# q and k of three heads ahead of the rest, seven products for every v, gate and SwiGLU pair, and a quad's first product copied into the bank of its second

## The chip, the cores and the metric

One core of a Trainium2 chip runs the kernel. The metric is the device time of one execution in microseconds (us). Engines: TensorE (PE), VectorE (DVE), ScalarE (ACT), GpSimd (POOL) and SyncE (SP, which issues most loads).

## What is computed

One layer of an encoder on x (512 tokens x 1024, float32), cut to its core:

```python
h = rmsnorm(x, g_mix)
xc, gb, gc, q, k, v, g_sw, gate_a, gate_r = split(h @ w_in)          # 1024 -> 3x1024, 1024, 1024, 2048, 2048, 1024, 1024
y_a = (gb * conv3(gc * xc)) @ w_a_out
q, k = rotary(q) * 256**-0.5, rotary(k)                              # 4 heads of 256; v: 4 heads of 512
ret  = retention(q, k, v, log_sigmoid(dec_f)) + reversed_strict_retention(q, k, v, log_sigmoid(dec_b))
y_r  = (groupnorm(ret) * g_ret * silu(g_sw)) @ w_r_out
x = x + (sigmoid(gate_a) * y_a + sigmoid(gate_r) * y_r) @ w_o
h2 = rmsnorm(x, g_ffn)
x = x + (silu(h2 @ w_ff_gate) * (h2 @ w_ff_up)) @ w_ff_down          # 1024 -> 2816 -> 1024
y = rmsnorm(x, g_final)
```

## The kernel before

Every operand of a matmul is split into a rounded high part and the rest (`split`: a cast on ACT, L171, and a subtraction on DVE, L172), and each product is three matmuls, high x high, high x low and low x high (`mm3`, L284 to L286; `prod`, L325, with 256 columns; `prod_tm`, L369, with 512). Weights come by SP's queue into `raw` tiles (10 buffers), and are split into `whi` and `wlo` (5 buffers of 128x1024, a "unit"), two units ahead of use. `plan()` lists the weights in the order of use. The order of instructions on each engine is that of a scheduler in the framework, which works from the program's order and the buffers; each engine then runs its own list in order.

A "quad" is a product of a 2x2 block matrix of activations and weights by Strassen's seven products: forms of the weights (b11, t1, t2, b21, t3, t4, b22) against forms of the activations (a11, s1, s2, a12, s3, a22, s4). A t-form of weights is made by DVE additions of two `raw` tiles (L244). `strassen` does it with 512 columns (v beside the gate of a head, the two branch gates, and w_ff_down), `fm_quad` with 256 (the convolution's inputs), `begin`, `second` and `pair` with 256 for SwiGLU. Three results are read while their bank goes on accumulating: ACT copies the bank to SBUF (`snap`, L376). The first product a11 is snapped too, and DVE adds it to a12's bank (L390, L339, L1018).

The order of the work: eight warm-up matmuls; v and gate of head 0 as plain products on x times gain, not yet normalised, since the reciprocal roots of the tokens (`rstd_tokens`, then `rstd_row` after the v product) are still computed; then x is normalised and the s-forms are made; q and k of head 0 (`do_qk`, rotated on DVE from PSUM by the table `rcs`); for heads 1 to 3 a quad for v and gate, and q and k; two quads for the branch gates; the decay tables (`decays`, with the logarithm `lgam` computed by small DVE steps on `lw`, L517 to L525, then Exp on ACT, L541); convolution, retention, output projections, w_o with a norm and transposes (`tr_o`, L910); SwiGLU, whose first pair of 256-column blocks is made by eight plain products (`first_pair`), the other ten by quads; w_ff_down in three parts; the last norm. v, gates, q and k are stored by POOL's queue (`store`, L566) from nine temporaries of 128x512 (`t512`).

## Time and profile before

| | us |
|---|---|
| runs | 1044.6 median of 3 (1043.32 to 1044.88) |
| profiled execution, its time | 1043.97 |
| its span, first to last instruction | 1042.2 |
| granted TensorE clock, mean | 0.998 |
| first matmul of the work | 6.67 |
| last matmul | 1033.33 |
| quad of head 1, 2, 3: start | 77.81, 137.65, 198.09 |

The span begins with the first instruction and ends with the last; 1.8 us of the execution's time lie around it. In a profile a line such as L369 is a line of the kernel; a helper's line stands for all that call it. Matmuls overlap, so the listed duration of one is longer than what it adds; the difference of the starts of neighbours is what it adds.

### The profile page before, as it was taken

To read this page: it belongs to the slowest core of one execution; us is meant where nothing else is said; L and a number is where in the kernel's file an instruction comes from. 1 tells how busy PE (TensorE), PEld (TensorE's weight loads), DVE (VectorE), ACT (ScalarE), POOL (GpSimd) and SP (SyncE) were. 2 spreads that over 40 slices of the span, in tenths; PEclk is the share of its full clock that TensorE was granted. 3 is DMA by queue.
4 is the path that set the end of the run, shared out by engine and by line. 5 is a ranking of instruction groups with operands and counts; after the bars stand their busy time and mean duration, and the time that the engine had idled before them with its cause. 6 is when DMAs were issued, how large, how long until landed. Compare 5 with 4: busy or idle time off the path is not lost.

```text
span 1042.2 us, 14832 instructions
## 1 busy us (share of the span) xinstructions
PE 1028.3 (99%) x5664; PEld 897.0 (86%) x5664; DVE 875.5 (84%) x1127; ACT 523.4 (50%) x698; POOL 107.7 (10%) x180
## 2 busy tenths in 40 slices
PE   8999999999999999999999999999999999999996
PEld 7788888888888998888888888889998999899985
DVE  6999786858787888697989998669998899889995
ACT  6546745452656545243443234355555565556553
POOL 0121111111111004202011000000002000110011
PEclk9999999999999999999999999999999999999999
DMA  9635638173645576919176535630319322663322
GB/s 325 223 117 201 236 123 281 71 254 119 199 141 182 169 284 233 341 42 358 42 283 247 205 111 173 236 113 28 92 45 275 117 85 78 193 152 102 122 35 87
DMA packets 49688, 175.07 MB, mean 168 GB/s; under 512 B 6480, under 2 KB 6480, under 8 KB 46288
## 3 DMA queue, kind: packets, MB, share of 16 engines
q1 hardware_dynamic: 36592, 131.12, 36.9%
q0 software_dynamic: 13024, 43.00, 12.9%
q8 instruction: 44, 0.72, 0.3%
q14 instruction: 28, 0.23, 0.1%
HBM read 135.56 MB, written 38.54 MB: 167 GB/s over the span
## 4 chain that ended last, share of the span: by engine, by line
PE 77%; issue 9%; DVE 7%; DMA 3%; POOL 2%; ACT 1%; SPq 0%; POOLq 0%; DVEq 0%; ACTq 0%
PE bank L369 29%; PE bank L325 27%; PE bank L285 7%; PE bank L284 7%; PE bank L286 7%; DVE wlo L172 1%; POOL z L566 1%; DVE big L185 1%; DMA big<-ql 1%; DMA big<-xT 1%; DMA z<-t 1%; DMA tab<-tab 0%; DVE big L172 0%; DVE t L464 0%; DVE big L175 0%
## 5 line engine op out<-in xcount | busy, mean ns | idle before, releaser
L171 ACT CAST whi<-raw 128x1024 fp32r<-128x1024 f32 (+1 forms) x281 | 288.6, 1032 | 302.7 <-PE bank L369 66.4
L172 DVE TENSOR_TENSOR wlo<-raw,whi 128x1024 fp32r<-128x1024 f32 (+1 forms) x281 | 335.8, 1202 | 108.8 <-ACT whi L171 107.8
L325 PE MATMUL bank<-xform,whi 128*128 128x256 f32 x1440 | 260.3, 283 | 0.0
L325 PEld LDWEIGHTS bank<-xform,whi 128*128 128x128 f32 x1440 | 224.8, 192 | 0.7 <-ACT t L376 0.6
L325 PE MATMUL bank<-xform,wlo 128*128 128x256 f32 x720 | 203.7, 283 | 0.0
L369 PE MATMUL bank<-whi,big 128*128 128x512 f32 x548 | 172.4, 390 | 0.0
L244 DVE TENSOR_TENSOR raw<-raw 128x1024 f32<-128x1024 f32 (+1 forms) x124 | 148.5, 1205 | 1.8 <-DMA raw<-wquad 0.4
L325 PEld LDWEIGHTS bank<-xform,wlo 128*128 128x128 f32 x720 | 138.2, 192 | 0.0
L369 PEld LDWEIGHTS bank<-whi,big 128*128 128x128 f32 x548 | 102.7, 188 | 22.4 <-DVE big L172 0.6
L369 PE MATMUL bank<-wlo,big 128*128 128x512 f32 x274 | 106.7, 389 | 0.0
L369 PE MATMUL bank<-whi,xform 128*128 128x512 f32 x320 | 101.2, 389 | 0.3 <-ACT t L376 0.3
L284 PE MATMUL bank<-whi,big 128*128 128x512 f32 x240 | 94.3, 395 | 1.8 <-ACT big L174 1.8
L285 PE MATMUL bank<-wlo,big 128*128 128x512 f32 x240 | 94.3, 393 | 0.0
L286 PE MATMUL bank<-whi,big 128*128 128x512 f32 x240 | 93.4, 392 | 0.0
L284 PE MATMUL bank<-big,whi 128*128 128x512 f32 x224 | 87.1, 389 | 0.0
L285 PE MATMUL bank<-big,whi 128*128 128x512 f32 x224 | 87.1, 389 | 0.0
L286 PE MATMUL bank<-big,wlo 128*128 128x512 f32 x224 | 87.1, 389 | 0.0
L376 ACT COPY t<-bank 128x512 f32<-128x512 f32 x96 | 55.5, 585 | 35.8 <-PE bank L369 17.2
L369 PEld LDWEIGHTS bank<-whi,xform 128*128 128x128 f32 x320 | 60.1, 188 | 13.1 <-ACT t L376 0.7
L369 PE MATMUL bank<-wlo,xform 128*128 128x512 f32 x160 | 62.2, 389 | 0.0
L369 PEld LDWEIGHTS bank<-wlo,big 128*128 128x128 f32 x274 | 51.4, 188 | 10.5
L284 PEld LDWEIGHTS bank<-whi,big 128*128 128x128 f32 x240 | 45.5, 190 | 12.5 <-ACT big L174 2.1
(173 smaller groups left out, 1398.6 us busy)
## 6 DMA issues: line engine op xcount, KB each, us to landing
raw<-wquad SPq DMA_DIRECT2D x124, 512.0 KB, 4.4
raw<-wpack SPq DMA_DIRECT2D x58, 512.0 KB, 4.9
z<-t POOLq DMA_DIRECT2D x24, 256.0 KB, 4.9
zform<-z POOLq DMA_DIRECT2D x6, 1024.0 KB, 6.2
v<-t POOLq DMA_DIRECT2D x16, 256.0 KB, 5.0
sg<-t POOLq DMA_DIRECT2D x16, 256.0 KB, 3.3
qh<-t POOLq DMA_DIRECT2D x16, 256.0 KB, 2.6
ql<-t POOLq DMA_DIRECT2D x16, 256.0 KB, 2.7
```

What stands on the lines that cost most here:

```text
L171: nc.scalar.copy(hi, src)
L172: nc.vector.tensor_tensor(out=lo, in0=src, in1=hi.bitcast(F32), op=ALU.subtract)
L185: nc.vector.transpose(o[:, :, :, b, :], i[:, :, :, q, :])
L244: nc.vector.tensor_tensor(out=t, in0=t, in1=raws[quad, more, u][:, 0:n], op=ALU.add)
L284: nc.tensor.matmul(ps, lh, rh, start=first, stop=False)
L285: nc.tensor.matmul(ps, lh, rl, start=False, stop=False)
L286: nc.tensor.matmul(ps, ll, rh, start=False, stop=last)
L325: nc.tensor.matmul(o, l[:, c], r[:, k], start=start and s == 0 and k == 0 and i == 0, stop=stop and k == 3 and i == 2, skip_group_check=True)
L369: nc.tensor.matmul(pss[tt], l, r[:, c], start=start and k == 0 and i == 0, stop=stop and k == n - 1 and i == 2, skip_group_check=True)
L376: nc.scalar.copy(t, ps)
L566: nc.gpsimd.dma_start(dst, t)
```

## The change

q and k of heads 0 to 2 are computed first, four banks to a head, on x times gain without the tokens' norm; ACT copies them to SBUF (`early`), and they are rotated later, half a head in each of the first six quads, by a table `rcn` that holds the tokens' norm too. v and gate of head 0 become a quad, as does SwiGLU's first pair. In each quad ACT copies a11's bank into another bank (`seed`), and a12 accumulates onto that copy; the addition on DVE is gone. The decay tables are made before the quads, with two tables of differences, eight Exps, and stores by POOL's queue. At the start the small columns come by ACT's queue, x ahead of weights, in larger transfers, and the first cast of weights is on DVE. The core of the diff, with a few comments put in:

```diff
@@ plan(): order of the weights
-    for c in (C_V, C_G):
+    for h in range(EARLY):                       # EARLY = 3
         for r in (0, 512):
-            b("w_in", r, 4, c, 512)
+            b("w_in", r, 4, (C_Q + h * QK, C_K + h * QK), 512)
     for h in range(HEADS):
-        if h:
-            quad(C_V + h * VD, C_G + h * VD)
-        a("w_in", C_Q + h * QK)
-        a("w_in", C_K + h * QK)
+        quad(C_V + h * VD, C_G + h * VD)
+        if h >= EARLY:
+            a("w_in", C_Q + h * QK)
+            a("w_in", C_K + h * QK)
...
-    f(0, "b11", "b21", "b12", "b22")
+    f(0, "b11", "b21")
     f(1, "b11", "b21")
+    f(2, "b11")
     for q0, n in FF_PARTS:
-        for q in range(max(q0, 1), q0 + n):
+        for q in range(q0, q0 + n):
...
-            if q + 1 < NQ:
+            if 1 < q < NQ - 1:
                 f(q + 1, "b11")
@@ prefetch_block()
-        for c in range(2 * per):
-            nc.sync.dma_start(st[c // per][:, c % per * m:(c % per + 1) * m], wpack[i][:, c * m:(c + 1) * m])
+        for c, (o, n) in enumerate(((0, 512), (512, 512), (QH, QH)) if pieces > 2 else ((0, QH), (QH, QH))):
             if loads:
                 loads(c)
+            nc.sync.dma_start(st[o // QH][:, o % QH:o % QH + n], wpack[i][:, o:o + n])
...
+                round = None if made else nc.vector.tensor_copy
+                made.append(split(st[half][:, sl], hi[:, sl], lo[:, sl], round=round))
@@ quads
+    def seed(ps, t=None):
+        t = t or bank()
+        nc.scalar.copy(t, ps)
+        return t
 def fm_quad(...):                                # strassen() likewise
-        a, d, b = bank(), bank(), bank()
+        a, d = bank(), bank()
         prod(w(), forms["a11"], a, True)
-        p1 = snap(a)
+        b = seed(a)
         prod(w(), forms["s1"], d, True)
         prod(w(), forms["s2"], a, False)
         u2 = snap(a)
-        prod(w(), forms["a12"], b, True)
-        nc.vector.tensor_tensor(out=p1, in0=b, in1=p1, op=ALU.add)
-        ev11(p1)
+        prod(w(), forms["a12"], b, False)
+        ev11(b)
@@ start
+    cols_sb = const.tile([P, N_COLS], F32, name="cols_sb")
+    nc.scalar.dma_start(cols_sb, cols)
...
-    prefetch(4, load_x, split_x)
+    prefetch(4, lambda c: load_x(c, 1 + c // 2), split_next)
+    prefetch(2, lambda c: load_x(4 + 2 * c, 2), lambda c: split_two(4 + 2 * c))
...
+    for h in range(EARLY):
+        pss = [bank() for _ in range(4)]
+        for kk in range(8):
+            if kk % 4 == 0:
+                c = Chunk()
+            if (h, kk) == (0, 7):
+                ss.rstd_tokens()
+            if (h, kk) == (1, 1):
+                rrow = snap(ss.rstd_row())
+                xg = quarters()                  # x times gain and rrow, and its split, as before
...
+            for m in range(4):
+                mm3(pss[m], c.w(kk % 4, m * P, P), act_pair(xu, kk), kk == 0, kk == 7)
+        t = bigtile()
+        for m in range(4):
+            nc.scalar.copy(t[:, m, :], pss[m])
+        early.append(t)
@@ decays: called before the four heads instead of after the gates' quads
+        for h in range(HEADS):
+            f, g = t512(), t512()
+            nc.scalar.activation(f, d[0], AF.Exp, scale=lgam[:, h:h + 1])
+            nc.scalar.activation(g, d[1], AF.Exp, scale=lgam[:, 4 + h:5 + h])
+            nc.vector.tensor_tensor(out=f[:, 0:P], in0=f[:, 0:P], in1=g[:, 384:512], op=ALU.mult)
+            store(tabs[h][:, 0:384], g[:, 0:384])
+            store(tabs[h][:, 384:896], f)
@@ rotation of the early heads: rcn = rcs * rrow, one half head in each quad
+    def turn_one():
+        if held:
+            h, j = held.pop(0)
+            rotate(h, j, early[h][:, 2 * j, :], early[h][:, 2 * j + 1, :], rcn)
...
+                if tt and o:                     # in do_quad's eviction of the sixth product
+                    turn_one()
     for h in range(HEADS):
-        if h:
-            do_quad(vd[h], sgd[h], AF.Silu)
-        do_qk(h)
+        do_quad(vd[h], sgd[h], AF.Silu)
+        if h >= EARLY:
+            do_qk(h)
@@ w_o: after the evictions of token blocks 1 and 3
+        if nb in (1, 3):
+            prefetch()
@@ SwiGLU (first_pair() is gone)
     def begin(q):
...
-        st["p1"] = snap(st["a"])
+        st["p1"] = seed(st["a"], (po[0][1], po[0][2], po[1][2])[q] if q < 3 else None)
     def second(q):
-        b = bank()
         _, (w,) = take()
-        prod(w, XF[1, 0], b, True)
-        g = heads_of[q]["p1"]
-        nc.vector.tensor_tensor(out=g, in0=b, in1=g, op=ALU.add)
+        prod(w, XF[1, 0], heads_of[q]["p1"], False)
     def pair(q):
...
-        if q + 1 < NQ:
+        if 1 < q < NQ - 1:
             begin(q + 1)
...
-    first_pair()
+    begin(0)
+    second(0)
+    tr_o(NB - 1, hs[NB - 1])
+    XF.update(sums(xf32[0, 0], xf32[1, 0], xf32[0, 1], xf32[1, 1]))
     begin(1)
     second(1)
+    begin(2)
     for q0, n in FF_PARTS:
-        for q in range(max(q0, 1), q0 + n):
+        for q in range(q0, q0 + n):
             pair(q)
@@ tail
-            put(held.pop())
+            with tc.issue_after(add.ins), tc.issue_after(square.ins):
+                put(held.pop())
```

How it moves instructions, at three places. On TensorE around the row of reciprocal roots: `bank<-t512,ones_r` (L493 before, L509 and L510 after) are the matmuls that spread the roots over the partitions. Before, the first of them follows straight on the first product that comes after the small `rstd_tokens` matmuls:

```order
L284 MATMUL bank_260<-whi_151,big_96 128x512
L285 MATMUL bank_260<-wlo_152,big_96 128x512
L286 MATMUL bank_260<-whi_151,big_98 128x512
L493 MATMUL bank_405<-t512_377,ones_r_83 128x512
L284 MATMUL bank_410<-whi_315,big_95 128x512
L285 MATMUL bank_410<-wlo_316,big_95 128x512
```

Afterwards, the second head's first matmuls stand ahead of it:

```order
L294 MATMUL bank_365<-big_96,wlo_281 128x512
L292 MATMUL bank_366<-big_96,whi_280 128x512
L293 MATMUL bank_366<-big_98,whi_280 128x512
L294 MATMUL bank_366<-big_96,wlo_281 128x512
L509 MATMUL bank_324<-t512_342,ones_r_85 128x512
L510 MATMUL bank_324<-t512_343,ones_r_85 128x512
L292 MATMUL bank_363<-big_96,whi_280 128x512
L293 MATMUL bank_363<-big_98,whi_280 128x512
```

Between the last `rstd_tokens` matmul and the first row matmul there are 12 matmuls of 512 columns before, and 24 after; the low half's matmul moves up to the high half's.

On ACT, at the start of the first quad of the program. Before (head 1's quad; the rows are the end of q and k of head 0, `t<-t` their rotated halves, and `t_800`, `t_802` the snaps of a11):

```order
46 L171 CAST xform<-big 128x1024
47 L171 CAST whi<-raw 128x1024 x2
48 L171 CAST t_655<-t_650 128x512
49 L171 CAST t_666<-t_661 128x512
50 L171 CAST whi<-raw 128x1024 x2
51 L171 CAST t_739<-t_734 128x512
52 L171 CAST whi<-raw 128x1024 x2
53 L171 CAST t_750<-t_745 128x512
54 L171 CAST whi<-raw 128x1024
55 L376 COPY t_800<-bank 128x512
56 L376 COPY t_802<-bank 128x512
```

After (head 0's quad): L531 and L532 are the Exps of the decays, L586 the copies of the early heads' banks, `xform` the s-forms, L340 the seeds. Just ahead of these rows stand two more Exps (36, 37) and, in row 35, the cast of t1's first unit:

```order
38 L531 ACTIVATE t_718<-t_705,lgam 128x512
39 L532 ACTIVATE t_719<-t_709,lgam 128x512
40 L531 ACTIVATE t_725<-t_705,lgam 128x512
41 L532 ACTIVATE t_726<-t_709,lgam 128x512
42 L531 ACTIVATE t_732<-t_705,lgam 128x512
43 L532 ACTIVATE t_733<-t_709,lgam 128x512
44 L586 COPY big<-bank 128x512 x2
45 L174 CAST xform<-big 128x1024
46 L586 COPY big<-bank 128x512 x2
47 L174 CAST xform<-big 128x1024 x3
48 L174 CAST whi<-raw 128x1024
49 L340 COPY bank<-bank 128x512 x2
```

Eight Exps, four copies and the casts of the four s-forms now stand between the cast of t1's first unit and that of its second, in row 48.

On TensorE in SwiGLU, from s2 (t2's product) to s3 (t3's). Before, in the first pair that is a quad, s2 is `bank_6221<-xform_6146` and the rows of `bank_6381` are the next pair's first product:

```order
L325 MATMUL bank_6221<-xform_6146,wlo_6251 128x256
L325 MATMUL bank_6221<-xform_6146,whi_6250 128x256 x2
L325 MATMUL bank_6221<-xform_6146,wlo_6251 128x256
L325 MATMUL bank_6381<-xform_5790,whi_6313 128x256 x2
L325 MATMUL bank_6381<-xform_5790,wlo_6314 128x256
L325 MATMUL bank_6381<-xform_5790,whi_6313 128x256 x2
```

After, in pair 0, s2 is `bank_5970<-xform_6045`, and s3, `xform_6041`, is the next row:

```order
L333 MATMUL bank_5970<-xform_6045,whi_6114 128x256 x2
L333 MATMUL bank_5970<-xform_6045,wlo_6115 128x256
L333 MATMUL bank_5970<-xform_6045,whi_6114 128x256 x2
L333 MATMUL bank_5970<-xform_6045,wlo_6115 128x256
L333 MATMUL bank_5970<-xform_6041,whi_6148 128x256 x2
L333 MATMUL bank_5970<-xform_6041,wlo_6149 128x256
```

The 13 matmuls of the next pair between s2 and s3 are gone there; between s3 and a22 stand 6 matmuls instead of 11. `begin(0)`, the copy and `second(0)` follow one another with nothing between.

More of the change, by code (lines that the diff above doesn't have):

```diff
@@ L177, in split @@
                 op0=ALU.mult, op1=ALU.subtract)
+        return first
     def transpose(out, src):
@@ L379, in strassen @@
     def strassen(n, forms, ev11, ev21, ev22, ev12):
-        a, d, b = ([bank(), bank()] for _ in range(3))
+        a, d = ([bank(), bank()] for _ in range(2))
         prod_tm(n, forms["a11"], a, True)
-        p1 = [snap(x) for x in a]
+        b = [seed(x) for x in a]
         prod_tm(n, forms["s1"], d, True)
@@ L498, in block_kernel, with decays @@
     for k in range(8):
-        ss.add(xs[k // 4][:, k % 4, :])
+        with tc.issue_after(made[min(k + 1, 3)].ins):
+            ss.add(xs[k // 4][:, k % 4, :])
     ss.split()
+    def decays():
+        d = []
+        for base, op in ((0, ALU.max), (-384, ALU.min)):
+            delta = t512(mybir.dt.int32)
+            nc.gpsimd.iota(delta, pattern=[[1, 512]], base=base, channel_multiplier=-1)
+            d.append(t512())
+            nc.vector.tensor_scalar(out=d[-1], in0=delta, scalar1=0.0, scalar2=None, op0=op)
+        for h in range(HEADS):
[5 more added lines that the diff above has]
+            store(tabs[h][:, 384:896], f)
@@ new lines, in keep, with store @@
+    def keep(dst, src):
+        hi, lo = t512(F32R), t512(F32R)
+        split(src, hi, lo)
+        for d, t in zip(dst, (hi, lo)):
+            store(d, t.bitcast(F32))
+    def store(dst, t):
+        nc.gpsimd.dma_start(dst, t)
+    rrow = None
+    early = []
+    for h in range(EARLY):
[8 more added lines that the diff above has]
+                xg = quarters()
+                for k in range(8):
+                    xk = xs[k // 4][:, k % 4, :]
+                    nc.vector.scalar_tensor_tensor(out=xk, in0=xk, scalar=gmix[:, k:k + 1], in1=rrow,
+                                                   op0=ALU.mult, op1=ALU.mult)
+                for i in range(2):
+                    for k in (0, 2):
+                        split(xs[i][:, k:k + 2, :], xg[0][i][:, k:k + 2, :], xg[1][i][:, k:k + 2, :])
+            for m in range(4):
[4 more added lines that the diff above has]
+        early.append(t)
@@ new lines, in form_tile, with sums @@
+    def form_tile():
+        t = big.tile([P, 2, 4, 256], F32R, tag="big", name="xform", padded_shape=[P, 2, 4, 256])
+        return t[:, 0], t[:, 1]
+    def sums(a11, a12, a21, a22):
+        out = {}
+        for name, o, in0, in1, op in (
+                ("s1", a22, a21, a22, ALU.subtract), ("s3", a21, a11, a21, ALU.subtract),
+                ("s2", a11, a22, a11, ALU.subtract), ("s4", a12, a12, a11, ALU.add)):
+            nc.vector.tensor_tensor(out=o, in0=in0, in1=in1, op=op)
+            out[name] = form_tile()
+            split(o, *out[name])
+        return out
@@ L503, in block_kernel @@
+    xf = sums(*(xs[i][:, :, o:o + 256] for o in (0, 256) for i in range(2)))
+    for n, i, o in (("a11", 0, 0), ("a12", 1, 0), ("a22", 1, 256)):
+        xf[n] = tuple(t[i][:, :, o:o + 256] for t in xg)
+    xforms = {n: of(t) for n, t in xf.items()}
     dec = const.tile([P, 8], F32, name="dec")
@@ L608, in block_kernel, with rotate @@
-    for n, i, o in (("a11", 0, 0), ("a12", 1, 0), ("a22", 1, 256)):
-        xf[n] = tuple(t[i][:, :, o:o + 256] for t in xg)
-    xforms = {n: of(t) for n, t in xf.items()}
+    def rotate(h, j, t1, t2, table):
+        cos, sin = table[:, 0, :], table[:, 1, :]
+        for i, (c1, c2, op) in enumerate(((cos, sin, ALU.subtract), (sin, cos, ALU.add))):
+            a, b = t512(), t512()
+            nc.vector.tensor_tensor(out=a, in0=t1, in1=c1, op=ALU.mult)
+            nc.vector.tensor_tensor(out=b, in0=t2, in1=c2, op=ALU.mult)
+            nc.vector.tensor_tensor(out=a, in0=a, in1=b, op=op)
+            keep([t[:, 2 * j + i, :] for t in qkd[h]], a)
@@ L612, in do_qk @@
+    rcn = misctile(D, "rcn").rearrange("p (i n) -> p i n", i=2)
+    for i in range(2):
+        nc.vector.tensor_tensor(out=rcn[:, i, :], in0=rcs[:, i, :], in1=rrow, op=ALU.mult)
+    held = [(h, j) for h in range(EARLY) for j in range(2)]
+    def turn_one():
+        if held:
+            h, j = held.pop(0)
+            rotate(h, j, early[h][:, 2 * j, :], early[h][:, 2 * j + 1, :], rcn)
     def do_qk(h):
@@ L1093, in to_y @@
         done[nb] += 1
+        return add, square
     def rms(nb):
```

160 lines of the change are left out of this document (42 added, 118 removed).

## The prediction

> **What bounds the kernel now.** I read the page's busy times first, then the list of waits of TensorE, then stretches of the timeline. One line of busy times:
>
> ```profile
> PE 1028.3 (99%) x5664; PEld 897.0 (86%) x5664; DVE 875.5 (84%) x1127; ACT 523.4 (50%) x698; POOL 107.7 (10%) x180
> ```
>
> TensorE is busy for 99% of the span of 1042.2 us. Everything that it waits for, in the list of its waits (bank, line <- releaser: us in total, times, longest):
>
> ```profile
> PE bank L284 <- ACT big L174: 1.8, 1, 1.8
> PE bank L493 <- ACT t L171: 1.7, 1, 1.7
> PE bank L415 <- DVE lw L508: 1.0, 1, 1.0
> PE bank L285 <- DMA big<-ql: 0.4, 1, 0.4
> PE bank L369 <- ACT t L376: 0.3, 1, 0.3
> ```
>
> These five rows add up to 5.2 us. So a matmul that is removed anywhere is worth its full spacing, as long as no new wait fills the place; and the only wait in mid-kernel worth removing is L493. The spacing is the difference of starts, not the listed duration, since neighbours overlap. Timeline of TensorE, start and duration in us, first for 512 columns and then for 256 ("x2" is two matmuls in one row):
>
> ```profile
> 499.77 0.39 PE L286 MATMUL bank<-whi,big 128*128 128x512 f32 x1
> ...
> 501.13 0.39 PE L286 MATMUL bank<-whi,big 128*128 128x512 f32 x1
> ...
> 733.72 0.28 PE L325 MATMUL bank<-xform,wlo 128*128 128x256 f32 x1
> 733.84 0.40 PE L325 MATMUL bank<-xform,whi 128*128 128x256 f32 x2
> ```
>
> 499.77 to 501.13 is six spacings (five matmuls stand between the two rows), 0.2267 us each; 733.72 to 733.84 is one, 0.120.
>
> **The change, term by term,** against the profiled execution (1043.97 us; the median of the runs is 1044.6, 0.6 above it).
>
> *Head 0's v and gate by seven products.* Two plain products of 96 matmuls (8 row blocks x 4 banks x 3) become seven of 24: 192 becomes 168. 24 x 0.2267 = **-5.44 us**. [...] q and k of heads 0 to 2 keep their 288 matmuls; they only move.
>
> *SwiGLU's first pair by seven products.* Eight products of 24 matmuls of 256 columns become seven. 24 x 0.120 = **-2.88 us**.
>
> *The row of reciprocal roots.* Now, on TensorE:
>
> ```profile
> 28.58 0.49 PE L284 MATMUL bank<-whi,big 128*128 128x512 f32 x1
> ...
> 31.21 0.39 PE L286 MATMUL bank<-whi,big 128*128 128x512 f32 x1
> 33.33 0.50 PE L493 MATMUL bank<-t,ones_r 128*128 128x512 f32 x1 [1.72 <-ACT t L171]
> ...
> 35.04 0.50 PE L494 MATMUL bank<-t,ones_r 128*128 128x512 f32 x1
> 35.38 0.39 PE L286 MATMUL bank<-whi,big 128*128 128x512 f32 x1
> ```
>
> From 31.21 to 35.38 lie eight spacings, which would take 1.81 and take 4.17: 2.36 lost. The chain that is waited for ends on ACT and DVE here:
>
> ```profile
> 32.66 0.62 ACT L171 CAST t<-t 128x512 fp32r<-128x512 f32 x1 [6.03 <-DVE lw L518]
> ...
> 34.30 0.68 DVE L172 TENSOR_TENSOR t<-t,t 128x512 fp32r<-128x512 f32 x1
> ```
>
> The hi half is there at 33.28, 4.7 us after 28.58. After the change 24 matmuls (5.44 us) stand between instead of 12, so the first of the two row matmuls finds its operand. The lo half comes 6.4 us after 28.58 now, but one us of that passes between the cast's end and the subtraction's start at 34.30, while DVE did other work; the small steps of the decays' logarithm no longer share DVE there. I take **-2.2**, between 0 (the lo half again late by a weight and a table's worth) and -2.36.
>
> *The first quad.* Durations by form that price this and what follows:
>
> ```profile
> L172 DVE TENSOR_TENSOR wlo<-raw,whi 128x1024 fp32r<-128x1024 f32 x270 | 328.4, 1223 | 101.9 <-ACT whi L171 101.0
> L171 ACT CAST whi<-raw 128x1024 fp32r<-128x1024 f32 x270 | 281.9, 1049 | 293.0 <-PE bank L369 64.7 <-PE bank L286 53.9 <-PE bank L325 45.7
> L376 ACT COPY t<-bank 128x512 f32<-128x512 f32 x96 | 55.5, 585 | 35.8 <-PE bank L369 17.2 <-PE bank L325 15.6 <-PE bank L286 2.5
> L619 DVE TENSOR_TENSOR t<-bank,rcs 128x512 f32<-128x512 f32 x16 | 11.0, 686 | 1.1 <-PE bank L286 1.1
> L525 DVE TENSOR_SCALAR lgam<-lgam 128x4 f32<-128x4 f32 x1 | 0.2, 170 | 0.0
> ```
>
> Let T be the end of the 288 early matmuls. ACT runs in its order: the cast of t1's first unit, eight Exps, four copies of the last early banks with four casts of forms, then the cast of t1's second unit (the order on ACT is shown with the change). The Exps wait for lgam, whose last steps on DVE stand behind that first unit. The unit's buffer comes free when the third head's second quarter is done, at T-10.9 (48 matmuls left). Then a cast of 1.05, a subtraction 1.22, an addition 1.22 and seven small steps of 0.2: T-6.0. Two Exps, at a copy's 0.59 each, bring T-4.8; the last Exp takes a buffer whose store must land first. The nearest stores, with us from issue to landing at the row's end:
>
> ```profile
> v<-t POOLq DMA_DIRECT2D x16, 256.0 KB, 5.0
> sg<-t POOLq DMA_DIRECT2D x16, 256.0 KB, 3.3
> qh<-t POOLq DMA_DIRECT2D x16, 256.0 KB, 2.6
> ```
>
> With 2.6 to 5.0 to land and 0.6 for the last Exp, ACT is free at T-1.6 to T+0.8. From there copies 4 x 0.59 and casts 4 x 1.05 take 6.5, and DVE needs two subtractions (2.4) more, for the fourth form and t1's second unit: 9.0 in all, where TensorE wants them at T+8.4 (36 matmuls and one). Lateness -1.0 to +1.4. I take **+1.2**, near the upper end, because t2's casts and subtractions stand behind these in the same two orders; bounds 0 to +4 (the late 1.4 again for t2, and an Exp or two). [...]
>
> *The quads' new load.* Each of six quads now carries one half head's rotation: eight DVE operations of 0.69 (5.5 us), less two additions (1.4). Both stretches below are TensorE at full work: one head's q and k with preparation of forms, and a quad (us, then busy time and count by engine: PE, PEld, DVE, ACT, POOL):
>
> ```profile
> 35.00:77.80 42.80, 42.76 (x188) 35.40 (x189) 41.51 (x45) 22.92 (x28) 7.62 (x13) 1.00 0.43 143
> 137.70:176.30 38.60, 38.30 (x169) 31.41 (x168) 28.95 (x32) 22.44 (x28) 6.42 (x12) 1.00 0.65 211
> ```
>
> A quad on DVE becomes 14 subtractions and 8 additions of weights (26.9), four of results (2.8) and the rotation (5.5): 35.2 in 38.1. DVE stood at 41.5 of 42.8 above without a wait of TensorE. The seeds on ACT take the place of snaps and have two products (10.9 us) before they are used. I count **0** (to +4), covered by DVE's remaining 2.9 us a quad.
>
> *The copies into banks where nothing stands between.* The last product of a kind that is read and then accumulated further, in a conv quad now, with six matmuls between:
>
> ```profile
> 348.41 0.28 PE L325 MATMUL bank<-xform,wlo 128*128 128x256 f32 x1
> ...
> 349.13 0.28 PE L325 MATMUL bank<-big,wlo 128*128 128x256 f32 x1
> 349.37 0.50 PE L325 MATMUL bank<-big,whi 128*128 128x256 f32 x2
> 349.71 0.28 PE L325 MATMUL bank<-big,wlo 128*128 128x256 f32 x1
> ```
>
> (Between the first two rows stand five matmuls, of another product.) The reading copy takes 0.59 (L376 above), and the bank is written again 0.96 after the last matmul's start; the two gaps cost 0.22 (349.13 to 349.71 is 0.58 for three spacings). Without the six it is 0.72 more, 0.94; with two, 0.70. By the new order: SwiGLU begin(0) goes straight into second(0), 0.94; in pair 0 s2 into s3, 0.94; s3 into a22 with six, 0.22; in pair 1 two, 0.70, and six, 0.22. In pair 0 the next pair's first weights (two matmuls put ahead) wait for the buffer of t1, just read, and a cast of 1.05, behind another: 1.3. Together **+4.3**, bounds +1.5 (only those the copy forces) to +6.5 (s1's form, which now has three products, 8.6 us, ahead of it instead of a whole pair, is late too). What goes from this stretch is a gap of 0.25, in place of 0.36 for three:
>
> ```profile
> 738.88 0.78 PE L325 MATMUL bank<-xform,whi 128*128 128x256 f32 x3
> 739.49 0.28 PE L325 MATMUL bank<-xform,wlo 128*128 128x256 f32 x1
> ```
>
> **-0.25**. The last conv quad loses seven score matmuls that stood between s3 and a22: **+0.72** (0 to 0.94).
>
> *Start, tail, table stores:* the first loads are bigger and x comes first, yet the same 2 MB (four row blocks of x and of weights) must land before the third and fourth block can be multiplied; 0, within about one copy of 0.6 either way. The eight table stores join a queue whose engine is 10% busy, and the last output store is moved behind an addition that waits for the last matmul anyway: 0.
>
> Sum: -5.44 - 2.88 - 2.2 + 1.2 + 4.3 - 0.25 + 0.72 = -4.55, so 1043.97 - 4.55 = **1039.4 us**.
>
> **The rivals.**
>
> *No new waits.* The scheduler's order keeps other work at all these places, or ACT answers faster: 1043.97 - 5.44 - 2.88 - 2.2 - 0.25 = 1033.2. For it speaks that TensorE is kept at 99% today; against it, the same copy already costs 0.22 behind six matmuls.
>
> *The temporaries hold DVE in the quads (the other side).* Rotation adds four stores a quad, all through nine temporaries of 128x512. A rotation row on DVE that waits for such a store holds the subtraction for t2's first unit, queued behind it; TensorE waits for that. From the end of the quad's last evictions the row comes 9.6 us after, where 11.1 are to be had: 1.5 to spare. A store of v lands 5.0 after issue, so a row held 3 us would cost 1.5 in each of six quads, 9 in all: 1048.4. It decides beyond 2.7 us. For: v's 5.0 against 2.6 of qh. Against: POOL is idle nine tenths of the time, and the list of waits names no store.
>
> *Upper bounds together in one place: pair 0.* If s1's form and first quad both come at their bounds, +2.2 and +2.8 on top: 1044.4, no change. For: DVE is at 95% in that stretch:
>
> ```profile
> 740.00:779.00 39.00, 39.00 (x288) 36.87 (x287) 37.24 (x49) 22.94 (x34) 0.00 (x0) 1.00 0.17 54
> ```
>
> *The row's wait stays.* The reciprocal row still waits, in another head: +2.2, 1041.6.
>
> **How the numbers follow.** The forecast's case 0.60 (1036.5 to 1042); no new waits 0.13; the row's wait stays 0.05; pair 0 and first quad at their bounds 0.13 (about 1042.5 to 1046); temporaries 0.09. Faster by over 0.2% (under 1042.5, about what can be told from no change at 1044.6) holds the first three, 0.78; same 0.13; slower 0.09. The range 1034 to 1045 leaves out most of the no-wait case and the temporaries.
>
> **What would show it.** Right: 24 fewer matmuls of each width; L509 without a wait; one gap of 1 to 2 us in the first quad on a weight or form; three gaps near 0.9 and one near 1.3 at SwiGLU's first two pairs, named after copies by ACT. Wrong: TensorE waits of over 1 us on DVE in the second to sixth quad, rotation rows on DVE that wait for DMAs, or a third row block at the start that waits for its load beyond 15 us.

## The result, and the profile after

The changed kernel takes 1038.12 us (median of 4 runs, 1036.39 to 1038.57), the kernel before 1044.11 (4 runs): ratio 0.9943, 95% interval 0.993 to 0.9956. That is 5.99 us, 0.57% faster; 1039.4 was forecast. The profiled execution took 1038.05 us with a span of 1036.3. One execution further down, one of b2, took 3046.7 us (a span of 3044.7 at a granted clock of 1.000), and is left out.

The page's line of busy times after:

```profile
PE 1021.7 (99%) x5616; PEld 890.2 (86%) x5616; DVE 878.9 (85%) x1121; ACT 541.1 (52%) x735; POOL 114.8 (11%) x189
```

48 matmuls fewer, and TensorE is still busy for 99%. The list of TensorE's waits after (bank, line <- releaser: us in total, times, longest):

```profile
PE bank L333 <- ACT t L390: 1.5, 3, 0.7
PE bank L333 <- ACT bank L340: 1.5, 1, 1.5
PE bank L292 <- DVE whi L174: 1.1, 1, 1.1
PE bank L430 <- DVE lw L616: 1.0, 1, 1.0
PE bank L333 <- ACT whi L174: 1.0, 1, 1.0
PE bank L383 <- ACT bank L340: 0.4, 1, 0.4
PE bank L383 <- DVE wlo L175: 0.4, 1, 0.4
PE bank L333 <- DVE xform L175: 0.2, 1, 0.2
```

The waits grew from 5.2 to 7.1 us, although the 1.7 of the reciprocal row are gone: new are six rows: three name ACT's copies (L390, and L340, the copy from bank to bank), one a cast of weights, two late lo halves. The list leaves out idle time that it does not put down to a releaser, so below I use the timeline: the difference of starts, less 0.227 us for 512 columns or 0.120 for 256.

TensorE's timeline after, places in the order of the program (start, duration in us):

```profile
5.97 1.62 PE L292 MATMUL bank<-big,whi 128*128 128x512 f32 x3 [1.15 <-DVE whi L174]
...
9.93 0.40 PE L292 MATMUL bank<-big,whi 128*128 128x512 f32 x1
...
26.99 0.17 PE L491 MATMUL bank<-ones_r,t 128*128 128x2 f32 x1
...
33.16 0.40 PE L294 MATMUL bank<-big,wlo 128*128 128x512 f32 x1
33.39 0.39 PE L509 MATMUL bank<-t,ones_r 128*128 128x512 f32 x1
...
82.62 0.61 PE L383 MATMUL bank<-whi,xform 128*128 128x512 f32 x2
83.60 0.50 PE L383 MATMUL bank<-wlo,xform 128*128 128x512 f32 x1 [0.36 <-DVE wlo L175]
...
340.61 0.28 PE L333 MATMUL bank<-big,wlo 128*128 128x256 f32 x1
341.32 0.51 PE L333 MATMUL bank<-big,whi 128*128 128x256 f32 x2 [0.43 <-ACT t L390]
...
696.37 0.28 PE L333 MATMUL bank<-xform,wlo 128*128 128x256 f32 x1
698.15 0.50 PE L333 MATMUL bank<-xform,whi 128*128 128x256 f32 x2 [1.50 <-ACT bank L340]
...
714.31 0.28 PE L333 MATMUL bank<-xform,whi 128*128 128x256 f32 x1
715.56 0.82 PE L333 MATMUL bank<-xform,whi 128*128 128x256 f32 x3 [0.97 <-ACT whi L174]
...
769.07 0.50 PE L383 MATMUL bank<-whi,big 128*128 128x512 f32 x1 [0.42 <-ACT bank L340]
```

The row of reciprocal roots (33.39) follows its neighbour by 0.23: no wait. The first quad waits once, 0.53 plus 0.10 for the slow first spacing behind it, on a lo half. The first quad of the convolution waits 0.59 plus 0.10 on a snap. SwiGLU's begin(0) and second(0) are 1.78 apart instead of the 0.96 that the copy in the conv quad of before took (348.41 to 349.37); where pair 0 waits for its borrowed weights the starts are 1.25 apart, with slow spacings behind.

What stands ahead of that copy, from ACT's timeline:

```profile
696.57 1.04 ACT L174 CAST whi<-raw 128x1024 fp32r<-128x1024 f32 x1 [0.53 <-PE bank L333]
697.52 0.58 ACT L340 COPY bank<-bank 128x512 f32<-128x512 f32 x1
```

A cast of weights that waited for TensorE started 0.2 us after the product's last matmul did; the copy stood behind it.

The end of the span, TensorE and then DVE after:

```profile
1028.74 0.39 PE L383 MATMUL bank<-whi,big 128*128 128x512 f32 x1
```

```profile
1029.16 0.69 DVE L1115 TENSOR_TENSOR big<-bank,big 128x512 f32<-128x512 f32 x1 [0.64 <-PE bank L383]
1029.77 0.74 DVE L1140 SCALAR_TENSOR_TENSOR big<-big,fin,gf 128x512 f32<-128x512 f32 x1
```

and before:

```profile
1033.33 0.39 PE L369 MATMUL bank<-whi,big 128*128 128x512 f32 x1
```

```profile
1034.79 0.75 DVE L1111 SCALAR_TENSOR_TENSOR big<-big,fin,gf 128x512 f32<-128x512 f32 x1 [0.65 <-POOL fin L1099]
1035.46 0.68 DVE L1087 TENSOR_TENSOR big<-bank,big 128x512 f32<-128x512 f32 x1
```

Before, the last addition (L1087) began 2.13 us after the last matmul's start, because DVE stood in front of it with a scaling that waited for POOL. After, it begins 0.42 after, and the scaling comes behind it. From the last matmul's start to the end of the span it is 8.87 before and 7.56 after.

The ledger, in us, by differences of starts in the two profiled executions (a row is good to 0.1 or 0.2):

| place | predicted | measured |
|---|---|---|
| 24 + 24 matmuls | -8.32 | -8.32 |
| start (first matmul 6.67, now 5.97) | 0 | -0.75 |
| row of reciprocal roots | -2.2 | -2.33 |
| first quad (+0.63; a wait of 0.57 in head 2's quad is gone) | +1.2 | +0.06 |
| quads 2 to 6 | 0 | 0 |
| convolution | +0.72 | +0.54 |
| SwiGLU, pairs 0 and 1 (0.43 before, 6.08 after) | +4.05 | +5.65 |
| w_ff_down, first part | not priced | +0.89 |
| a load of q's lo half (-0.70), w_o (+0.34) | not priced | -0.36 |
| tail | 0 | -1.3 |
| sum | -4.55 | -5.92 |

### The profile page after: what moved, and what is told of

It reads as the page before. It is cut to its first block, busy times and chain, and to the rows that moved or that the text cites. A ratio compares the mean times of both kernels' runs of the same rounds, so it can differ in the third digit from the quotient of the medians.

```text
span 1036.3 us, 14743 instructions
## 1 busy us (share of the span) xinstructions
PE 1021.7 (99%) x5616; PEld 890.2 (86%) x5616; DVE 878.9 (85%) x1121; ACT 541.1 (52%) x735; POOL 114.8 (11%) x189
## 4 chain that ended last, share of the span: by engine, by line
PE 65%; issue 22%; POOL 5%; DVE 5%; ACT 2%; DMA 1%; POOLq 0%; SPq 0%; ACTq 0%; DVEq 0%
PE bank L333 23%; PE bank L383 13%; PE bank L294 10%; PE bank L292 10%; PE bank L293 9%; DVE wlo L175 1%; DVE raw L252 1%; POOL sg L559 1%; POOL v L559 1%; POOL qh L559 1%; POOL ql L559 1%; ACT whi L174 1%; DVE big L600 1%; POOL tab L559 0%; POOL lw L617 0%
## 5 line engine op out<-in xcount | busy, mean ns | idle before, releaser
L175 DVE TENSOR_TENSOR wlo<-raw,whi 128x1024 fp32r<-128x1024 f32 (+1 forms) x290 | 344.2, 1199 | 98.5 <-ACT whi L174 97.8
L383 PE MATMUL bank<-whi,big 128*128 128x512 f32 x596 | 188.0, 390 | 0.5 <-ACT bank L340 0.4
L252 DVE TENSOR_TENSOR raw<-raw 128x1024 f32<-128x1024 f32 (+1 forms) x136 | 161.6, 1203 | 1.4
L383 PEld LDWEIGHTS bank<-whi,big 128*128 128x128 f32 x596 | 111.6, 188 | 25.5 <-ACT bank L340 0.9
L383 PE MATMUL bank<-whi,xform 128*128 128x512 f32 x384 | 121.2, 389 | 0.0
L383 PE MATMUL bank<-wlo,big 128*128 128x512 f32 x298 | 116.0, 389 | 0.0
L383 PEld LDWEIGHTS bank<-whi,xform 128*128 128x128 f32 x384 | 72.1, 188 | 15.0
L383 PE MATMUL bank<-wlo,xform 128*128 128x512 f32 x192 | 74.8, 390 | 0.4 <-DVE wlo L175 0.4
L292 PE MATMUL bank<-whi,big 128*128 128x512 f32 x176 | 69.0, 392 | 0.0
L293 PE MATMUL bank<-wlo,big 128*128 128x512 f32 x176 | 68.5, 389 | 0.0
L294 PE MATMUL bank<-whi,big 128*128 128x512 f32 x176 | 68.2, 390 | 0.1
L390 ACT COPY t<-bank 128x512 f32<-128x512 f32 x77 | 45.0, 585 | 43.0 <-PE bank L333 21.0
L292 PEld LDWEIGHTS bank<-big,whi 128*128 128x128 f32 x224 | 42.5, 190 | 10.2 <-ACT big L177 1.4
```

What stands on the lines that cost most here:

```text
L175: nc.vector.tensor_tensor(out=lo, in0=src, in1=hi.bitcast(F32), op=ALU.subtract)
L252: nc.vector.tensor_tensor(out=t, in0=t, in1=raws[quad, more, u][:, 0:n], op=ALU.add)
L292: nc.tensor.matmul(ps, lh, rh, start=first, stop=False)
L293: nc.tensor.matmul(ps, lh, rl, start=False, stop=False)
L294: nc.tensor.matmul(ps, ll, rh, start=False, stop=last)
L383: nc.tensor.matmul(pss[tt], l, r[:, c], start=start and k == 0 and i == 0, stop=stop and k == n - 1 and i == 2, skip_group_check=True)
```

## The experiments

My theory after the result: the matmuls saved are worth their spacing; head 0's seven products pay, SwiGLU's first pair costs more than it saves, because copies on ACT stand bare between products; the copies as seeds bring nothing by themselves; the tail's new order is a gain that I had not priced. The rivals were, for each part, that it does the opposite or nothing. The runs a, b and c were made on three different chips, each beside the kernel before (1043.71, 1043.29 and 1042.7 us); across the letters, compare ratios.

**a1, the tail alone undone.**

```diff
-            with tc.issue_after(add.ins), tc.issue_after(square.ins):
-                put(held.pop())
+            put(held.pop())
```

> Only the tail's order is undone: the last output's store and scaling may again be issued ahead of the last addition. Theory: the changed kernel's tail (7.6 us from the last matmul's start to the end of the span, against 8.9 before) is shorter because DVE no longer holds the last addition behind a scaling that waits for POOL; then this run is 1.3 us longer than the changed kernel, 1039.4. Rival: the tail is shorter for another reason (a store that lands sooner), and nothing changes: 1038.1.

Measured: 1038.27 (1038.17 to 1038.33), ratio 0.9947 (0.9932 to 0.9962). Its last matmul and the last addition:

```profile
1027.02 0.39 PE L383 MATMUL bank<-whi,big 128*128 128x512 f32 x1
```

```profile
1028.49 0.75 DVE L1140 SCALAR_TENSOR_TENSOR big<-big,fin,gf 128x512 f32<-128x512 f32 x1 [0.65 <-POOL fin L1128]
1029.16 0.68 DVE L1115 TENSOR_TENSOR big<-bank,big 128x512 f32<-128x512 f32 x1
```

The addition is 2.14 behind the matmul's start again, with the scaling in front, and the tail takes 9.2 us (to 1036.2) against 7.56. So the mechanism stands and is worth 1.65 us here. The total alone hides it: 1038.27 is as long as the changed kernel's 1038.12. This kernel reached its last matmul 1.72 us sooner, and that came entirely from the start: its first two-column matmul (L491), after 84 large ones, began at 25.26 where the changed kernel's began at 26.99. That is the start, which differs from run to run (see b1 and the end). By the ratios it is 1.7 us slower than the control b1 (0.9947 against 0.9931), but the intervals overlap: what shows the mechanism is the order on DVE and the tail's length, not the total.

**b1, the changed kernel once more,** as a control on another chip.

> The changed kernel once more, beside the others, to see how far its own runs spread. In the traces so far TensorE leaves half rate 2.1 to 4.0 us after its first matmul of the work, which makes up to 1.7 us of difference between runs of one kernel. Theory: that is all of the spread (1036.4 and 1038.1 as two groups). Rival: other waits move too, and the groups do not follow the start.

Measured: 1036.32 (1035.73 to 1037.73), ratio 0.9931 (0.9911 to 0.995). Its start, on TensorE's timeline:

```profile
5.78 0.94 PE L292 MATMUL bank<-big,whi 128*128 128x512 f32 x3 [0.96 <-DVE whi L174]
...
7.95 0.39 PE L292 MATMUL bank<-big,whi 128*128 128x512 f32 x1
```

Nine matmuls in 2.17 us here, 3.96 in the profile of the changed kernel above (5.97 to 9.93); full spacing would be 2.04. In a1 and a4 they take 2.14 and 2.16: the 2.1 us that the expectation gives to half rate are nine matmuls close to full spacing, and the slow ones, at 0.43, stand in the other profiles. The program is the same. (The profile of before has the slow start too.) The last matmul comes 2.66 us sooner here; 2.01 of that lie ahead of the first two-column matmul, and 0.64 in the first quad, which waits for nothing in this profile. So the start makes most of the difference, where the theory had it make all, and one other wait moves too, as the rival had it. A total moves by over 2 us with no cause in the code, and terms of 1 us are read from the timeline, at one place, not from totals.

**a2, SwiGLU's first pair plain again,** eight products, with the first product of the next pair inside each pair as before.

```diff
-    f(0, "b11", "b21")
-    f(1, "b11", "b21")
-    f(2, "b11")
+    f(0, "b11", "b21", "b12", "b22")
+    f(1, "b11", "b21")
...
-            if 1 < q < NQ - 1:
+            if q + 1 < NQ:
                 begin(q + 1)
...
-    begin(0)
-    second(0)
+    first_pair()                      # eight products, as in the kernel before
```

> SwiGLU's first pair again by eight plain products, with the next pair's first product inside each pair; the copies into banks stay. Theory: in the changed kernel TensorE loses 6.1 us in pairs 0 and 1 and 0.9 more than before in the first part of w_ff_down, where it lost about 0.5 in this stretch before, and all of that is for want of other products to put between; so undoing costs 2.9 of matmuls and gives back about 6: 1035 or so. Rival: the waits are those of the copies themselves and stay, and only the 2.9 of matmuls come back: 1041.

Measured: 1034.82 (1034.05 to 1035.77), ratio 0.9912 (0.9894 to 0.993). It has 24 matmuls more than the changed kernel and is no slower. From 640 us on, TensorE loses 3.7 us here and 8.7 in the changed kernel: 5.0 less for 2.9 of added matmuls, a net 2.1. The output of this kernel is not right (its copies go into other banks than the changed kernel's; why it is off was not found out), so its times stand only for this order of instructions, not for a version to use.

**a3, the first products of pairs 0 and 1 ahead of the second ones** (begin(0), begin(1), the last transposes, second(0), second(1), begin(2)).

```diff
-    f(0, "b11", "b21")
-    f(1, "b11", "b21")
+    f(0, "b11")
+    f(1, "b11")
+    f(0, "b21")
+    f(1, "b21")
...
     begin(0)
-    second(0)
+    begin(1)
     tr_o(NB - 1, hs[NB - 1])
     XF.update(sums(...))
-    begin(1)
+    second(0)
     second(1)
```

> SwiGLU's order changed only: the first products of pairs 0 and 1 follow one another, then the last transposes, then their second products. Theory: the 1.77 us between the first and the second product of pair 0 are the time of a weight cast and the copy on ACT with nothing between; with a product (2.9 us) between, they go: 1036.4. Rival: ACT's order puts the copy later still, or the s-form, which now has as much ahead of it as before, comes later and takes the time back: 1038.

Measured: 1036.07 (1035.34 to 1036.9), ratio 0.9926 (0.9911 to 0.9942). The gap of 1.78 is gone, but a later one is longer:

```profile
734.86 0.28 PE L335 MATMUL bank<-xform,wlo 128*128 128x256 f32 x1
736.54 0.51 PE L335 MATMUL bank<-xform,whi 128*128 128x256 f32 x2 [1.40 <-ACT t L392]
```

and in w_ff_down one gap of 1.3 takes the place of several that came to 1.2. From 640 us on it loses 7.7 against 8.7: one us, where the theory had 1.7. It looks as if the stretch, early by one gap, ran into the next one; no run here isolates that.

**a4, all gaps filled:** a3, and in each of pairs 0 to 3 a whole product of a later pair between s2 and s3.

```diff
-        if q > 1:
-            second(q)
+        if q in (1, 3):
+            begin(q // 2 + 3)
+        else:
+            second({0: 2, 2: 3}.get(q, q))
...
-        if 1 < q < NQ - 1:
+        if 3 < q < NQ - 1:
             begin(q + 1)
```

> As the run with the first products ahead, and between s2 and s3 of pairs 0 to 3 stands a whole product of a later pair. Theory: the copies' latency is all that is lost there, so the gaps of 0.94 and 0.70 and part of the wait of 1.4 for a weight go too: about 1034.5. Rival: the five weight buffers and DVE, which is at 95% there, set the pace; the gaps come back as waits for weights, and the run is at 1036.4 or above.

Measured: 1033.36 (1031.98 to 1034.88), ratio 0.9901 (0.9883 to 0.9918). In its list of waits L337, the 256-column products, has one row of 0.4 in place of four rows and 4.2:

```profile
PE bank L387 <- ACT big L178: 1.0, 1, 1.0
...
PE bank L337 <- ACT t L394: 0.4, 1, 0.4
```

The row of 0.4 lies in the convolution (338.62); what is left behind it is 1.2 in SwiGLU and 2.4 in w_ff_down's first part (L387). From 640 us on TensorE loses 5.3 here, against 3.7 in a2 with 24 matmuls (2.9) more: so by the two traces seven products for the first pair do pay, 1.3 us, once something stands between a product and its continuation. The totals (1033.36 and 1034.82) agree, but their intervals overlap.

**b2, no copies into banks:** ACT copies a11 to SBUF, a12 goes into a bank of its own, and DVE adds, in every quad.

```diff
-        b = seed(a)
+        p1 = snap(a)
...
-        prod(w(), forms["a12"], b, False)
-        ev11(b)
+        prod(w(), forms["a12"], b, True)
+        nc.vector.tensor_tensor(out=p1, in0=b, in1=p1, op=ALU.add)
+        ev11(p1)
```

> All copies of a first product into another bank are undone: ACT copies it to SBUF and DVE adds the second product's bank, as before; everything else of the change stays. Theory: the copies into banks save nothing where two products lie between (DVE and ACT had the time), and cost 1.8 us where none lies between (SwiGLU's pair 0), so undoing them gives about 1036.4. Rival: the 20 additions (0.6 us each) that DVE was spared are what lets it carry the rotations and seven products, and waits for DVE appear in the quads: 1039 or more.

Measured: 1034.95, 1034.8 and 1036.3; ratio 0.9917 (0.9898 to 0.9936) against the control's 0.9931. The profile is of the execution that is left out, so no place can be read. The median is 1.4 us below the control, the intervals overlap: no gain of the copies is seen, and they may cost a little. The rival's 1039 is excluded: in this order TensorE can do with the additions on DVE. c1 has the places.

**b3, head 0's v and gate by plain products.**

```diff
+    for c in (C_V, C_G):
+        for r in (0, 512):
+            b("w_in", r, 4, c, 512)
...
-            quad(C_V + h * VD, C_G + h * VD)
+            if h:
+                quad(C_V + h * VD, C_G + h * VD)
```

> v and gate of head 0 by two plain products again (192 matmuls instead of 168), after the three heads' q and k, on normalised x; the rest of the change stays, one half head's rotation stands by itself. Theory: a matmul costs its spacing, so 24 x 0.2267 = 5.4 us more, less the 0.6 that the first quad waits for a weight: 1042.9. Rival: the plain products give DVE and ACT air that the quads lack, and less than 4 us is lost: under 1042.

Measured: 1042.65 (1041.2 to 1044.74, 10 runs), ratio 0.9988 (0.9977 to 0.9999): 6.3 above the control. In the profiles the last matmul is 9.2 us later than the control's. 3.8 of that lie ahead of the first two-column matmul (28.80 against 24.98): a first matmul 1.05 later and the slow start. 5.4 remain, which is 24 matmuls of 0.2267. That term of the prediction is shown.

**b4, the decay tables after the gates' quads,** as in the kernel before.

```diff
-    decays()                          # ahead of the heads' quads
     for h in range(HEADS):
         do_quad(vd[h], sgd[h], AF.Silu)
...
+    decays()
     mix_quads()
```

> The decay tables (eight Exps, their stores) are made after the gates' quads again, in their new form. Theory: the 0.63 us that the first quad waits for t1's second weight is ACT's time for the eight Exps (5.0 us) ahead of the copies and casts; it goes: 1037.5. Rival: the casts of forms and the copies alone hold it, or the Exps now hold the first conv quad's copy, and nothing is gained: 1038.1 or more.

Measured: 1044.17 (1040.41 to 1045.09, 10 runs), ratio 1.000 (0.9987 to 1.0013): 7.9 above the control. The first quad has no gap left but 0.11; the control has none there either, with the Exps ahead, so this does not show that the Exps made the 0.63. The price has moved and grown. TensorE, ACT, and the stretch 339.8 to 345.1 us (busy time and count by engine, then granted clock, DMA share, GB/s):

```profile
334.92 0.28 PE L333 MATMUL bank<-big,wlo 128*128 128x256 f32 x1
339.83 0.80 PE L333 MATMUL bank<-xform,whi 128*128 128x256 f32 x2 [4.63 <-ACT t L390]
```

```profile
338.58 0.72 ACT L532 ACTIVATE t<-t,lgam 128x512 f32<-128x512 f32 x1 [2.12 <-DMA tab<-t]
339.21 0.56 ACT L390 COPY t<-bank 128x512 f32<-128x512 f32 x1
```

```profile
339.80:345.10 5.30, 5.27 (x24) 5.28 (x25) 3.50 (x3) 2.81 (x3) 0.86 (x2) 0.50 0.60 195
```

The Exps stand on ACT in front of the copy (L390) that frees the bank; the last one waits 2.12 for a table's store to land; TensorE waits 4.79 in all. Then it runs at 0.21 a matmul of 256 columns instead of 0.12 from 340.2 to 345.3, 5.1 us, 2.2 of them lost, with the granted clock at 0.50. With a further wait of 1.27 in the second conv quad (at 367.57) that makes up most of the 8.3 us that b4 loses against the control from the first two-column matmul on. This is the collision that the prediction feared for the first quad. There the Exps stand in front of copies too, but no Exp waited for a store.

**c1, a4 and b2 together.**

> All gaps filled in SwiGLU's first pairs (as a4) and, on top, no copies into banks (as b2). Theory: b2's gain over the changed kernel was the copy with nothing behind it, which a4 has removed by order; but a copy into a bank also holds the second product in w_ff_down's first part (0.7 us there), so a little is left: 1032 to 1033 against 1033.4. Rival: the copies spare DVE additions that the denser order needs: 1034.5 or more, with waits for DVE in pairs 0 to 3.

Measured: 1032.35 (1031.01 to 1033.48), ratio 0.9895 (0.9875 to 0.9914): about 11 us under the kernel before (0.0105 of its 1042.7), and the lowest median here, though a4's interval overlaps. One wait is new:

```profile
711.04 0.39 PE L337 MATMUL bank<-xform,wlo 128*128 128x256 f32 x1 [1.92 <-DVE wlo L179]
```

DVE, which does the additions again, is late with a lo half, and matmuls from 711.7 to 715.1 come at 0.21 instead of 0.12 (granted clock 0.50 from 711.7 to 715.0). c1 and a4 differ by the copies into banks alone, so their two profiles, compared place by place, give the copies' price. Without the copies TensorE loses 0.6 less in the convolution (0.65 against 1.24), 0.3 less in w_o, 2.1 less in w_ff_down's first part (0.36 against 2.44) and 0.6 less behind it; and 3.4 more in SwiGLU (4.61 against 1.17), which is this wait and the slow matmuls behind it. So both theories saw something: the copies cost 3.6 at four places, and at one place DVE is late without them (the wait of 1.92). With one profile each, it is not shown that this wait comes in every execution.

**c2, two half heads to a quad** (rotation in three quads instead of six).

```diff
                     turn_one()
+                    turn_one()
```

> Two half heads are rotated in each of the first three quads instead of one in each of six: DVE's work there rises from 35.2 to 40.7 us in a quad's 38.1. Theory: one rotation a quad is near the limit, so TensorE now waits for DVE in the second and third quad, 2 to 6 us in all. Rival: what DVE is late with one quad it makes good in the next, from weights split two units ahead: under 1 us of new waits.

One execution, 1038.88. New in the list of waits:

```profile
PE bank L383 <- DVE wlo L175: 1.1, 2, 0.7
PE bank L383 <- ACT whi L174: 0.5, 2, 0.3
```

(Of the first row, 0.4 is the wait in the first quad that the changed kernel's profile has too.) In the second and third quad TensorE loses 2.8 us that it does not lose with one half head each, as the theory had it. So the 2.9 us that the prediction left DVE in a quad, after one rotation of 5.5, do not hold a second one. In the convolution c2 loses 0.6 us less than the changed kernel (0.60 against 1.24): there DVE has no rotation to do in the sixth quad, just ahead.

**c3, the row of reciprocal roots after 12 matmuls again.**

```diff
-            if (h, kk) == (1, 1):
+            if (h, kk) == (1, 0):
```

> The row of reciprocal roots is asked for at the first of the second head's row blocks again, 12 matmuls after the small ones instead of 24. Theory: the chain through POOL, DVE and ACT takes 4.7 us to the high half and 6.4 to the low, so TensorE waits about 2 us before the row matmuls, as before the change. Rival: with the decays' logarithm no longer on DVE at that time the chain is short enough for 12 matmuls and a few: under 1 us.

One execution, 1036.22. TensorE and DVE:

```profile
28.84 0.39 PE L292 MATMUL bank<-big,whi 128*128 128x512 f32 x1
```

The next matmul, the row's first, starts here:

```profile
29.33 0.50 PE L509 MATMUL bank<-t,ones_r 128*128 128x512 f32 x1
```

```profile
26.15 0.16 DVE L495 TENSOR_SCALAR rtokv<-bank 128x4 f32<-128x4 f32 x1 [1.04 <-PE bank L492]
27.54 1.02 DVE L501 TENSOR_SCALAR t<-ident,rtok 128x128 f32<-128x128 f32 x4 [1.23 <-POOL rtok L498]
...
29.68 0.69 DVE L175 TENSOR_TENSOR t<-t,t 128x512 fp32r<-128x512 f32 x1
```

and DVE before, at the same work:

```profile
28.90 1.22 DVE L172 TENSOR_TENSOR wlo<-raw,whi 128x1024 fp32r<-128x1024 f32 x1
...
30.11 0.15 DVE L479 TENSOR_SCALAR rtokv<-bank 128x4 f32<-128x4 f32 x1
```

The wait is 0.26, 0.37 with the slow spacing behind it, where it was 2.36 before; the theory had about 2. The rival was right: what DVE no longer does at that time takes away 2.0 of it by itself. Before, DVE turned to the sums at 30.11, 2.34 after the two-column matmuls began (27.77); here it turns to them after 0.98 (from 25.17). In front of the sums stood a weight's subtraction (28.90), with steps of the decays' logarithm around it; these 1.36 us are nearly all by which the cast of the high half comes sooner (32.66, 4.89 after the two-column matmuls, before; 3.48 after them here). From the first of the four diagonals to that cast it is 1.20 before (from 31.46), with steps of the logarithm between, and 1.11 here (from 27.54): 0.1. The lo half starts 4.51 us after the two-column matmuls here, 6.53 before (34.30): another 0.6 went behind the cast. How much of this is the logarithm and how much the new place of the weights' subtractions is not separated.

The run does not show that the 24 matmuls are idle, either. By the rows of before, 12 more matmuls (2.72 us) would alone have covered the high half's wait of 1.88 and left, by my estimate, 0.6 for the low half (ready at 34.98, wanted at 34.39). Each of the two changes is nearly enough.

**c4, the start as before** (order of loads, sizes of transfers, first cast on ACT, no order put on the sums of squares).

> The start of before: columns, x and weights by SP's queue in 256 KB pieces with the weights first, and the first cast on ACT; all else as changed. Theory: the first matmul of the work comes 0.7 us later (6.67 against 5.97), and nothing else moves, since the same 2 MB must land: 0.7 us more than the changed kernel on the same chip. Rival: the later start is caught up by the third row block, which waits for its load either way: no difference.

Measured: 1037.59 (1037.06 to 1039.09), ratio 0.9947 (0.9931 to 0.9963), by the ratios 1.7 above the control, with intervals that overlap. The list of waits has the two rows that make the difference:

```profile
PE bank L292 <- ACT big L177: 1.9, 1, 1.9
PE bank L294 <- DVE wlo L175: 0.4, 1, 0.4
```

The first matmul comes at 6.77 instead of the control's 5.78, and a later row block waits for a lo half and the casts behind, 0.8 in all with the slow spacings around it. Both kernels had the quick start in their profiles, and the first two-column matmul stands at 26.81 against 24.98: 1.8. In the other six profiles with the quick start and the new loads it stands between 24.93 and 25.39, so the old start costs 1.4 to 1.9 up to there. The theory's 0.7 is too small: "nothing else moves" was wrong, as the later row block shows.

## Why the prediction was right, point by point

- *What bounds.* Right: TensorE at 99%, and a removed matmul worth its spacing (b3: 5.4 for 24 of 512 columns).
- *The row of reciprocal roots.* -2.2 forecast, -2.33 measured. The prediction gave the gain to the 24 matmuls in between and named DVE's other work second. c3 shows that DVE's part alone brings 2.0; by the estimate there the matmuls alone would have brought about as much. Which of two sufficient causes comes first cannot be said.
- *The first quad.* +1.2 forecast, +0.63 in this profile and nothing in the control's; the choice near the upper end was too much. The path to it was not right either: the sum has two Exps and a last one that "takes a buffer whose store must land first". In the trace the eight Exps run one behind the other (70.06 to 74.98, 0.61 apart) and none waits for a store. ACT is free 0.3 after the quad's start (74.69), inside the forecast's -1.6 to +0.8, and that is luck. In the control the same Exps end 0.9 ahead of the quad's start. In b4 an Exp waited for a store, 2.12 us, and that is part of the 4.79 there. That a wait of 0.57 in another quad would go was not foreseen.
- *The quads' new load.* Right, 0 in the second to sixth quad; c2, with two half heads to a quad, loses 2.8 there.
- *The convolution.* This step failed, and the number agrees by luck. +0.72 was forecast for the last quad, for want of seven score matmuls; they still stand there (381.40 to 383.07), and 0.15 is lost against 0.20 before. The +0.54 arose in the first quad (0.69 against 0.22 before) and at 352.28 (0.17). In the first, a cast that waited for a t-form from DVE stood on ACT in front of the copy:

```profile
339.73 1.05 ACT L174 CAST whi<-raw 128x1024 fp32r<-128x1024 f32 x1 [2.63 <-DVE raw L252]
340.69 0.58 ACT L390 COPY t<-bank 128x512 f32<-128x512 f32 x1
```

  Both the rotation in the sixth quad and the copies into banks are needed for it: c2, without the one, and c1, without the other, lose 0.60 and 0.65 in the convolution, like the kernel before (0.64).
- *SwiGLU's first pairs.* +4.3 forecast, 6.08 measured. All six places were there, and five had about their size (0.94, 0.22, 0.70 and 0.22 as forecast, 1.42 for 1.3). begin(0) to second(0) was priced at the copy's own 0.94 and took 1.76, as ACT's order puts a cast in front of the copy: the order on ACT had to be walked there as it was for the first quad. s1's form was late by 0.44, and 0.37 fell at 706.31, inside the upper bound.
- *Not priced:* w_ff_down's first part, +0.89, and w_o, +0.34; the seeds of w_ff_down's banks wait in the same way (769.07), and c1, without copies into banks, has 0.36 and 0.40 at these two places, no more than the kernel before (0.62 and 0.39).
- *The tail.* This step failed. "Moved behind an addition that waits for the last matmul anyway: 0" looked at the store and its scaling only. The scaling in front of the addition waited for POOL, so the addition was late, and everything behind it. a1 shows 1.65 us.
- *The signs.* 24 fewer matmuls of each width, no wait at L509 and gaps named after copies by ACT came as said. The gap of 1 to 2 us in the first quad did not (0.63), and of "three gaps near 0.9" one was (0.93); the others were 1.76 and 0.70.
- *The rivals.* No new waits: false, SwiGLU's alone are 6 us. Temporaries hold DVE in the quads: it happens, once, and costs nothing. At the end of head 3's quad a rotation row waits for a store of v, which the prediction had named as a sign of being wrong:

```profile
228.03 0.69 DVE L640 TENSOR_TENSOR t<-big,rcn 128x512 f32<-128x512 f32 x1 [1.57 <-DMA v<-t]
```

  Such a row stands in every profile of a changed version but c2's, with waits of 0.8 to 3.1 us (the longest in c3); TensorE loses nothing in quads 2 to 6 here, as the forecast's 1.5 to spare allows. Pair 0 and the first quad at their bounds: not together. The row's wait stays: no.

So the total came within 1.4 us of the profiled execution because an unpriced gain (tail 1.3, start 0.75, a load 0.70, the first quad 1.1 better) was a little larger than an unpriced loss (SwiGLU 1.6, w_ff_down 0.9, w_o 0.3). That these balanced is luck; what held is the matmuls' price, the row, and most of SwiGLU's gaps.

## What to carry to other kernels

Saving a product on a full TensorE paid its spacing here (5.4 us for 24 matmuls of 512 columns in b3) only where its new neighbours left time for what lies between: a bank that was read by a copy was written again 0.96 us after its last matmul's start, eight matmuls of 256 columns, and another product put there turned a loss of some 2 us (a2) into a gain of 1.3 (a4). Walk the in-order queue of the engine that does the reading (ACT here) at each such place, since here a cast (1.05 us) or an Exp (0.71) in front of the copy took longer than the copy (0.58). At the end of a kernel order the last operations by what waits for the last matmul, and put what waits for another engine behind it (here a scaling that waited for POOL: 1.65 us in a1).

## What the runs showed of the hardware

**The start has one of two speeds in these profiles.** In five of them (before, after, a2, a3, b3) the first matmuls of the work come at 0.43 us, for 3.1 to 6 us; in the others (a1, a4, b1, b4, all of c) the first is 0.31 to 0.34 ahead of the second, and from there on they come at 0.23. The slow start costs 1.5 to 2.8 us, 1.8 with the same program on both sides (after and b1). That it is also most of the spread between executions without a profile is not shown. The clock in the profile is 1.00 in either case (after from 5.9 to 10 us, a1 and a4 from 6 to 12), so only the spacing tells it. The matmuls come at 0.23 from 6.1 us on in b1, from 9.9 in the changed kernel, from 12.9 in b3. What decides this no run here shows; after and b1 differ in it with the same program, so the program alone does not. In c2 the warm-up matmuls ahead of the work end sooner too: at 4.44 us (6.04 less the wait of 1.60), where they end at 4.82 in the changed kernel (5.97 less 1.15).

**Behind two of these four waits in mid-kernel the matmuls came slowly.** Waits of 1.66 (after, up to 698.15) and 1.88 (before, up to the row at 33.33) were followed by full spacing; 2.07 in c1 by 3.4 us of matmuls at 0.21 instead of 0.12, 4.79 in b4 by 5.1 us. Here, other than at the start, the clock column shows it: 0.50 in both stretches. What sets the two pairs apart is not shown, and chance is not excluded; where it happened, c1's wait cost about 1.5 us more than its length (16 matmuls of 0.09).
